# The end of the hybrid layer: gate projection in its own group, norm factor in the last scan step, three more attention units in written order

## The chip, the cores and the metric

One core of a Trainium2 chip runs the whole program. The metric is the device time of one execution in microseconds (us); several executions are given by their median. The engines are named as the profile names them: PE (TensorE, matmuls), DVE (VectorE), ACT (ScalarE), POOL (GpSimd) and SP (SyncE, which issues most DMAs).

## What is computed

Two layers act on 512 latent tokens and 256 context tokens of width 1024. The first layer (hybrid) has two branches that share one input and one output projection: a bidirectional state-space scan of 16 heads in 4 groups, and a 2-D neighbourhood attention of 8 heads, which the kernel takes in 4 pairs. The second layer is a differential attention. Each layer ends in a gated MLP. The change is in the hybrid layer alone:

```python
def hybrid_mixer(ux, uc, w_in, ..., w_out, with_ctx):
    z_x, xbc_x, dt_x, q_x, k_x, v_x = parts(ux @ w_in)
    z_c, xbc_c, dt_c, q_c, k_c, v_c = parts(uc @ w_in)
    y_x, y_c = ssd_branch(...)
    a_x = neighbourhood_attention(q_x, k_x, v_x, k_c, v_c, rpb)
    ox = concatenate([y_x, a_x]) @ w_out

def gate_norm(y, z):                       # end of ssd_branch
    y = y.reshape(b, n, SSD_INNER) * silu(z)
    return rms_norm(y, norm_w)             # y * rsqrt(mean(y*y) + eps) * norm_w
```

The scan works in 6 chunks of 128 tokens (4 latent, 2 context). A chunk's output is a decay-weighted product inside the chunk plus what the states before it bring in from either direction.

## The kernel before

Weights are fp32. `wchunk` (line 156) loads a piece, ACT writes its high part and DVE (or POOL) its low part, and every dense product is three matmuls: high by high, high by the input's low part, low by high. On PE these show as px and pc (128x512 latent and 128x256 context columns, `ct_x`, `ct_c`, line 328), pz (the gate, `tc_mm`, line 344) and po (the output projection).

The hybrid layer is written as four rounds, one for a group g of four scan heads. In a round `run` takes the generators of `gens` in turn, one step each: `ssd_group(g)`, the scan, and from round 1 on `na_pair(g - 1)`, an attention pair of six units of 128 queries. After every second turn it takes one step of the filler, the dense work of later groups: `dense_ssd(g + 1)`, `x_rows(g + 1)`, `dense_na(g)` and `dense_z(g + 1)`, in this order. In round 3 the filler is `dense_na(3)` and `early()`, which loads the finished scan output (yr), transposes it (ytp), splits it in high and low parts (act tiles) and starts the output projection. The writing order gives each instruction a priority; a scheduler then orders each engine's queue by it, so that filler stands where the scan and the attention wait. What the filler of round 3 issues has its priority lowered by 4000.

One step of the scan (lines 673 to 712) reads a tile E of decays that POOL has loaded (`load_E`: a DMA, line 649, and two selects, lines 650 and 652), takes eight exponentials on ACT (line 681), eight products with dt on DVE (684, 685) and a product with the chunk's C B matrix (688, called M below), and then the four matmuls of line 706, which are called the chunk's products below. E, the scan's states, the inputs of the layer (`u`, 12 tiles) and the act tiles (12) share one pool, `blk`, of 18 buffers; so three are left for E in a round, and act tiles can be had only as E tiles and `u` come free. Line 711 squares and sums the gated output into ssq.

An attention unit (`na_unit`) makes scores on PE, adds the bias and takes the maximum on DVE, the exponential on ACT, the reciprocal and the scaling on DVE, the transposes on PE (line 108, S<-P), their copies on ACT or DVE (Pt, line 788) and the product with V on PE. Units 0 to 3 are latent, 4 and 5 context.

After the four rounds the norm factor rr is made (lines 949 to 952: a sum and a scale on DVE, a square root on ACT, a reciprocal and a scale on DVE). Then pair 3 runs with PE's order written out by hand (`pe.chain = True`): its q and k are split (`split_qk`, lines 746 to 752, to which five tiles of one buffer each belong) and V is transposed, and then each unit's three stages alternate with one `piece()`, that is one step of `rest()`: a group of 18 po matmuls and its evacuation by DVE and POOL.

Of the kernel before, what the change touches and what calls it, by code (L numbers as in the profile page):

```python
# [10 lines left out]
F32 = mybir.dt.float32  # L11
# [3 lines left out]
OP = mybir.AluOpType  # L15
# [59 lines left out]
def emit(tc, T):  # L75
# [546 lines left out]
    def ssd_group(g, BC, xs):  # L622
        Bc, Cc = BC
        hs = slice(4 * g, 4 * g + 4)
        Bt = sp.tile([128, 6, 128], F32, name="Bt", bufs=1)
        for c0, cn in ((0, 4), (4, 2)):
            p = pss.tile([128, 4, 128], F32, name="btp", tag="ax")
            for c in range(cn):
                nc.tensor.transpose(p[:, c], Bc[:, 128 * (c0 + c):128 * (c0 + c) + 128], ident)
            nc.scalar.copy(Bt[:, c0:c0 + cn], p[:, 0:cn])  # L630
        yield
        PVb = [blk.tile([128, 2, 2, 4, 64], F32, name="PV", tag="b") for _ in range(3)]
        PV = [PVb[k // 2][:, k % 2] for k in range(5)]
        wsg = wst.rearrange("p c (d h) -> p c d h", d=2)
        sdg = sd.rearrange("p c (d h) -> p c d h", d=2)
        b4 = [128, 2, 4, 64]

        def scaled(c, w, name, eng):
            xd = sp.tile([128, 2, 4, 64], F32, name=name, tag="f2", bufs=4)
            eng.tensor_tensor(xd, xs[c].rearrange("p (h q) -> p h q", q=64).unsqueeze(1).to_broadcast(b4),  # L640
                              w[:, c, :, hs].unsqueeze(3).to_broadcast(b4), op=OP.mult)
            return xd

        Es = {}

        def load_E(c):
            E = blk.tile([128, 2, 4, 128], F32, name="E", tag="b")
            base = scr[g, c].rearrange("d h l -> (d h l)")
            nc.gpsimd.dma_start(E.rearrange("p d h l -> p (d h l)"), base.unsqueeze(0).to_broadcast([128, 1024]))
            nc.gpsimd.affine_select(out=E[:, 0], in_=E[:, 0], pattern=[[0, 4], [1, 128]], compare_op=OP.is_ge,  # L650
                                    fill=NEG, base=0, channel_multiplier=-1)
            nc.gpsimd.affine_select(out=E[:, 1], in_=E[:, 1], pattern=[[0, 4], [-1, 128]], compare_op=OP.is_ge,
                                    fill=NEG, base=0, channel_multiplier=1)
            Es[c] = E

        for c in FO[:E_AHEAD[g]]:
            load_E(c)

        xw = {}
        for k in range(5):  # L660
            for c in (FO[k], BO[k]):
                if c not in xw:
                    xw[c] = scaled(c, wsg, "xw", nc.gpsimd)
            p = pss.tile([128, 2, 256], F32, name="Sps", tag="ax")
            nc.tensor.matmul(p[:, 0], Bt[:, FO[k]], xw[FO[k]][:, 0].rearrange("p h q -> p (h q)"), start=True, stop=True)
            nc.tensor.matmul(p[:, 1], Bt[:, BO[k]], xw[BO[k]][:, 1].rearrange("p h q -> p (h q)"), start=True, stop=True)
            pv = PV[k].rearrange("p d h q -> p d (h q)")
            if k == 0:
                nc.scalar.copy(pv, p)
            else:  # L670
                nc.gpsimd.tensor_tensor(PV[k], PV[k - 1], cdk[:, k, :, hs].unsqueeze(3).to_broadcast(b4), op=OP.mult)
                nc.vector.tensor_tensor(pv, pv, p, op=OP.add)
            yield
        for c in (4, 5, 0, 1, 2, 3):
            if c not in Es:
                load_E(c)
            E = Es.pop(c)
            for d in range(2):
                for h in range(4):
                    i = 16 * d + 4 * g + h  # L680
                    nc.scalar.activation(E[:, d, h], E[:, d, h], AF.Exp, bias=acs[:, c, i:i + 1])
            M = E[:, 0]
            for h in range(4):
                nc.vector.tensor_scalar(E[:, 1, h], E[:, 1, h], dt[:, c, 16 + 4 * g + h:17 + 4 * g + h], None, op0=OP.mult)
                nc.vector.scalar_tensor_tensor(M[:, h], M[:, h], dt[:, c, 4 * g + h:4 * g + h + 1], E[:, 1, h], op0=OP.mult, op1=OP.add)
            gp = pss.tile([128, 512], F32, name="gp", tag="ax")
            nc.tensor.matmul(gp[:, 0:128], Bc[:, 128 * c:128 * c + 128], Cc[:, 128 * c:128 * c + 128], start=True, stop=True)
            nc.vector.tensor_tensor(M, M, gp[:, 0:128].unsqueeze(1).to_broadcast([128, 4, 128]), op=OP.mult)
            kf, kb = FO.index(c), BO.index(c)
            op_ = pss.tile([128, 2, 256], F32, name="op", tag="ax")  # L690
            t1 = sp.tile([128, 2, 4, 64], F32, name="t1", tag="f2", bufs=4)
            ds_ = [d for d, k in ((0, kf), (1, kb)) if k > 0]
            for d in ds_:
                k = (kf, kb)[d]
                nc.tensor.matmul(op_[:, d], Cc[:, 128 * c:128 * c + 128], PV[k - 1][:, d].rearrange("p h q -> p (h q)"), start=True, stop=True)
            d0, d1 = ds_[0], ds_[-1] + 1
            nc.vector.tensor_tensor(t1[:, d0:d1], op_[:, d0:d1].rearrange("p d (h q) -> p d h q", q=64),
                                    sdg[:, c, d0:d1, hs].unsqueeze(3).to_broadcast([128, d1 - d0, 4, 64]), op=OP.mult)
            xD = sp.tile([128, 4, 64], F32, name="xD", tag="xD", bufs=2)
            nc.gpsimd.tensor_tensor(xD, xs[c].rearrange("p (h q) -> p h q", q=64),  # L700
                                    dsum[:, hs].unsqueeze(2).to_broadcast([128, 4, 64]), op=OP.mult)
            for d in ds_:
                nc.gpsimd.tensor_tensor(xD, xD, t1[:, d], op=OP.add)
            dg = gp[:, 128:384].rearrange("p (h q) -> p h q", q=64)
            for h in range(4):
                nc.tensor.matmul(dg[:, h], M[:, h], xs[c][:, 64 * h:64 * h + 64], start=True, stop=True)
            nc.vector.tensor_tensor(xD, xD, dg, op=OP.add)
            yf = xD.rearrange("p h q -> p (h q)")
            nc.vector.tensor_tensor(yf, yf, zs.pop((g, c)), op=OP.mult)
            nc.gpsimd.dma_start(scrY[c, :, 256 * g:256 * g + 256], yf)  # L710
            nc.scalar.activation(t1[:, 0].rearrange("p h q -> p (h q)"), yf, AF.Square, accum_out=ssq[:, c, g:g + 1])
            yield


# [45 lines left out]
    def na_unit(Q, Kh, Kl, V, qo, k0, chunks, bias, out, pool, tp_, nb, split=False):  # L760
# [55 lines left out]
                pe.matmul(av[hp], V[0:m, c, hp], Ss[e][1][0:m, i], start=(i == 0), stop=(i == len(chunks) - 1))  # L816
        out(av)

    def na_values(v):
        V = np_.tile([128, 7, 128], F32, name="V")  # L820
        for grp in ((1, 2, 3, 5), (6, 0, 4)):
# [22 lines left out]
            return na_unit(*QK, V, 128 * k, k0, chunks + (5, 6), bt, lambda av: na_out(p, 128 * k, av), pool, tp_, nb, split)  # L844
        return na_unit(*QK, V, 128 * k, None, (5, 6), None, lambda av: na_out(p, 128 * k, av), pool, tp_, nb, split)

    def na_pair(p, q, k, v, pools, nb=2):
        QK = split_qk(q, k)
        V = na_values(v)
        yield  # L850
        for u_ in range(6):
            bt = na_bias(p, u_, np_, nb) if u_ < 4 else None
            for _ in na_one(p, u_, QK, V, bt, pools[u_ % 4 % len(pools)], np_, nb):
                pass
            yield
# [19 lines left out]
    PNA = (pna, "na")  # L875
    dense, densen, rows, zs = {}, {}, {}, {}
    bg[:] = [(0, w, h) for w in (2, 4, 3) for h in range(2)]
    for _ in chain(dense_ssd(0), dense_z(0), x_rows(0)):
        pass
    acts, atts, Yt, pend = {}, {}, {}, []  # L880

# [48 lines left out]
    for g in range(4):  # L930
# [1 line left out]
            pmm.seq = MM  # L932
        gens = [ssd_group(g, *rows[g])]
        if g > 0:
            gens.append(na_pair(g - 1, *densen[g - 1], [(nring, None) if g == 3 else PNA]))
        fl = []
        if g < 3:
            fl += [dense_ssd(g + 1), x_rows(g + 1)]
        fl.append(dense_na(g))
        if g < 3:  # L940
            fl.append(dense_z(g + 1))
        if g == 3:
            fl.append(early())
        run(gens, chain(*fl), 4000 if g == 3 else 0)
# [1 line left out]
    pmm.seq = MM + [(pm3, "mm")]  # L946
    while bg:
        fill()
    ssr = sp.tile([128, 6], F32, name="ssr")
    nc.vector.tensor_reduce(ssr, ssq, axis=AX, op=OP.add)  # L950
    nc.vector.tensor_scalar(ssr, ssr, 1.0 / D, RMS_EPS, op0=OP.mult, op1=OP.add)
    nc.vector.tensor_scalar(rr, rsqrt_(ssr, sp), 1.0 / ALPHA, None, op0=OP.mult)
    s1.close()
    s4 = ExitStack()
    op4 = s4.enter_context(tc.tile_pool(name="op4", bufs=1))
# [67 lines left out]
    def piece():  # L1023
        pr = tc.cur_priority
        tc.cur_priority = pr + 4000
        next(rs_, None)
        tc.cur_priority = pr

    bts = [na_bias(3, b, np2, 4) for b in range(2)]
    QK3 = split_qk(*N[:2])  # L1030
    V3 = na_values(N[2])
    for tt in range(6):
        load_res(tt)
    evac_y()
    pe.chain = True
    prev = None
    for k in range(6):
        if 0 < k < 3:
            bts.append(na_bias(3, k + 1, np2, 4))
        un = na_one(3, k, QK3, V3, bts[k] if k < 4 else None, (PNA, (pss, "ax"))[k % 2], np2, 4, True)  # L1040
        next(un)
        if prev is not None:
            next(prev)
        piece()
        if prev is not None:
            next(prev, None)
        prev = un
# [518 lines left out]
```

## Time and profile before

| | |
|---|---|
| median of 3 runs | 2026.2 us (2025.8 to 2028.28) |
| the profiled execution's own time | 2025.07 us |
| its span | 2023.3 us |
| PE busy | 1920.8 us (95%) |
| DVE, ACT, POOL busy | 1352.1, 920.5, 769.6 us |
| chain that ended last | PE 72%, DVE 12%, DMA, POOL and ACT 4% each |

PE is busy nearly everywhere, so time can be won only where it is idle or runs at a low granted clock. The page's 40 slices show such places at the start, at some 490 to 560 us (the end of the hybrid layer) and at 700 to 760 us (the start of the first MLP). A view of the windows gives these stretches one by one.

### The profile page before, as it was taken

How to read it: one execution, taken by the hardware profiler on the slowest of the kernel's cores; microseconds unless marked ns; L12 is line 12 of the kernel's file. 1: busy time of each engine (PE TensorE's matmuls, PEld its weight loads, DVE VectorE, ACT ScalarE, POOL GpSimd, SP SyncE). 2: the span in 40 equal slices, each digit the busy share in tenths (PEclk: the TensorE clock that was granted, in tenths of full speed). 3: DMA queues.
4: the chain of work that ended last, by engine and by line, in shares of the span. 5: the costliest groups of instructions: out<-in, count | busy, mean ns of one | idle time of the engine just before them, and what ended most of it. 6: DMA issues, size and time to landing. Idle time of an engine off the chain costs nothing.

```text
span 2023.3 us, 31146 instructions
## 1 busy us (share of the span) xinstructions
PE 1920.8 (95%) x11928; PEld 1645.3 (81%) x11928; DVE 1352.1 (67%) x2172; ACT 920.5 (45%) x1799; POOL 769.6 (38%) x658
## 2 busy tenths in 40 slices
PE   7998999998699889999999999899999899999997
PEld 5887889887477788878888888899998788888886
DVE  3757565765556887887676667566665876655566
ACT  3545466585442732323222234656665644333332
POOL 2135224336315675444444408431115264222133
PEclk9999999999699989999999999999999999999999
DMA  9335342233422243433343342222122223323321
GB/s 314 113 114 170 110 129 76 96 117 117 155 68 88 87 135 100 130 116 115 105 144 106 104 135 86 92 73 85 55 66 68 89 64 126 104 84 104 103 96 62
DMA packets 109445, 217.59 MB, mean 108 GB/s; under 512 B 27112, under 2 KB 45904, under 8 KB 109296
## 3 DMA queue, kind: packets, MB, share of 16 engines
q1 hardware_dynamic: 95168, 187.87, 28.9%
q0 software_dynamic: 6016, 20.03, 2.8%
q10 hardware_dynamic: 8112, 7.71, 1.3%
q8 instruction: 94, 1.54, 0.3%
q14 instruction: 55, 0.45, 0.1%
HBM read 202.81 MB, written 8.55 MB: 104 GB/s over the span
## 4 chain that ended last, share of the span: by engine, by line
PE 72%; DVE 12%; DMA 4%; POOL 4%; ACT 4%; issue 3%; ACTq 0%; SPq 0%; DVEq 0%; POOLq 0%
PE fpx L328 20%; PE pdn L1122 11%; PE px L328 7%; PE fpc L328 5%; PE S L108 3%; PE po L108 3%; PE pc L328 3%; PE pz L344 3%; DVE acc L223 2%; PE pv L344 2%; DMA araw<-in_ada_w 2%; POOL y L409 2%; PE dSp L1329 2%; PE po L1005 2%; PE pk L328 2%
## 5 line engine op out<-in xcount | busy, mean ns | idle before, releaser
L172 ACT ACTIVATE whi<-raw 128x1024 fp32r<-128x1024 f32 (+1 forms) x203 | 213.4, 1056 | 443.5 <-PE fpc L328 167.2
L173 DVE TENSOR_TENSOR wlo<-raw,whi 128x1024 fp32r<-128x1024 f32 (+1 forms) x190 | 251.8, 1330 | 157.4 <-ACT whi L172 144.6
L352 POOL TENSOR_TENSOR y<-y,ev 128x512 f32<-128x512 f32 x144 | 212.5, 1495 | 185.1 <-DVE ev L350 175.2
L1122 PE MATMUL pdn<-whi,fact 128*128 128x512 f32 x880 | 273.1, 392 | 2.1 <-DVE ev L350 1.8
L328 PE MATMUL fpx<-ux,whi 128*128 128x512 f32 (+1 forms) x832 | 232.3, 363 | 8.2 <-DVE cv L1081 7.6
L328 PE MATMUL fpx<-u,whi 128*128 128x512 f32 (+1 forms) x832 | 226.5, 358 | 2.4 <-DVE cv L1081 1.5
L1122 PEld LDWEIGHTS pdn<-whi,fact 128*128 128x128 f32 x880 | 162.4, 188 | 37.2 <-DVE ev L350 2.9
L328 PEld LDWEIGHTS fpx<-ux,whi 128*128 128x128 f32 x832 | 150.3, 194 | 31.1 <-ACT whi L172 8.0
L1122 PE MATMUL pdn<-wlo,fact 128*128 128x512 f32 x440 | 170.8, 390 | 0.7 <-DVE wlo L173 0.7
L328 PEld LDWEIGHTS fpx<-u,whi 128*128 128x128 f32 x832 | 149.2, 191 | 25.1 <-ACT cv L1077 1.6
L328 PE MATMUL fpx<-ux,wlo 128*128 128x512 f32 (+1 forms) x416 | 151.1, 364 | 8.5 <-POOL wlo L173 6.6
L223 DVE SCALAR_TENSOR_TENSOR acc<-araw,condp,acc 128x512 f32<-128x512 f32 x140 | 137.4, 1002 | 24.4 <-DMA araw<-in_ada_w 24.0
L1106 POOL TENSOR_TENSOR fact<-cv,fact 128x768 fp32r<-128x768 f32 (+1 forms) x44 | 70.6, 1605 | 217.5 <-ACT fact L1105 217.5
L328 PE MATMUL fpx<-u,wlo 128*128 128x512 f32 (+1 forms) x416 | 148.8, 358 | 1.1 <-DVE wlo L173 1.1
L328 PE MATMUL px<-ux,whi 128*128 128x512 f32 x448 | 148.5, 405 | 0.0
L171 POOL TENSOR_TENSOR raw<-raw,G 128x1024 f32<-128x1024 f32 x30 | 74.4, 2482 | 193.0 <-DMA raw<-in_w_down 113.0
L1081 DVE SCALAR_TENSOR_TENSOR cv<-fpx,fcw,cv 128x511 f32<-128x511 f32 x176 | 130.3, 744 | 20.8 <-ACT cv L1077 19.6
L328 PE MATMUL fpc<-uc,whi 128*128 128x256 f32 x704 | 130.2, 283 | 0.0
L328 PEld LDWEIGHTS fpc<-uc,whi 128*128 128x128 f32 x704 | 112.6, 191 | 4.2 <-issue 0.6
L409 POOL TENSOR_TENSOR y<-y,gb 128x256 f32<-128x256 f32 x112 | 98.9, 918 | 35.2 <-PE lntp L388 28.7
L1077 ACT ACTIVATE cv<-fpx,fcw 128x512 f32<-128x512 f32 x88 | 67.8, 771 | 80.7 <-PE fpx L328 76.5
L350 DVE SCALAR_TENSOR_TENSOR ev<-pdn,G 128x512 f32<-128x512 f32 x120 | 81.3, 683 | 32.0 <-POOL y L352 18.9
(335 smaller groups left out, 4628.0 us busy)
## 6 DMA issues: line engine op xcount, KB each, us to landing
araw<-in_ada_w SPq DMA_DIRECT2D x96, 512.0 KB
raw<-in_w_up SPq DMA_DIRECT2D x88, 512.0 KB
raw<-in_w_down SPq DMA_DIRECT2D x44, 512.0 KB
E<-scr POOLq DMA_DIRECT2D x24, 512.0 KB, 5.4
raw<-in_w_dqk SPq DMA_DIRECT2D x16, 512.0 KB
raw<-in_w_qkv SPq DMA_DIRECT2D x12, 512.0 KB
raw<-in_w_out SPq DMA_DIRECT2D x12, 512.0 KB
raw<-in_w_bc SPq DMA_DIRECT2D x8, 512.0 KB
```

What stands on the lines that cost most here:

```text
L108: i = f(*a, **k)
L171: nc.gpsimd.tensor_tensor(raw, raw, gate, op=OP.mult)
L172: nc.scalar.activation(hi[:, :n], raw[:, :n], AF.Copy)
L173: i = (eng or nc.vector).tensor_tensor(lo[:, :n], raw[:, :n], hi[:, :n].bitcast(F32), op=OP.subtract)
L223: nc.vector.scalar_tensor_tensor(acc[:, s], raw[:, i], cs, acc[:, s], op0=OP.mult, op1=OP.add)
L328: nc.tensor.matmul(ps, w[wi][:, kc], rhs(kc, ui), start=(i == 0), stop=(i == n - 1))
L344: nc.tensor.matmul(ps, u_dst(u, kc, ui, tt), w(kc, wi), start=(i == 0), stop=(i == n - 1))
L350: nc.vector.scalar_tensor_tensor(t, ps, r, Gh, op0=OP.mult, op1=OP.mult)
L352: eng.tensor_tensor(yh, yh, t, op=OP.add)
L409: i = nc.gpsimd.tensor_tensor(y[:, c:c + 256], y[:, c:c + 256], t[:, c:c + 256], op=op)
L1081: nc.vector.scalar_tensor_tensor(dst[:, lo:hi_], src[:, lo + d:hi_ + d], f[:, tap:tap + 1], dst[:, lo:hi_], op0=OP.mult, op1=OP.add)
L1122: nc.tensor.matmul(ps, acts[2 * gs[0] + kt][:, ui, 128 * tt:128 * tt + 128], ws[kt][wi][:, 0, o:o + 512], start=(m == 0), stop=(m == 3 * n ...
```

## The change

Four edits, all in the hybrid layer.

- The gate's projection of a group, `dense_z(g)`, is the first filler of round g instead of the last filler of round g - 1. The sequence of the filler is the same; what moves is where the rounds' scans and attention pairs begin against it. In round 3 this leaves `dense_z(3)`, `dense_na(3)` and `early()`.
- The norm factor is written inside the last step of the last scan instead of behind the rounds.
- Pair 2 runs only its units 0 to 2 in round 3 (`n=3`); units 3 to 5 run behind the rounds in the order written out by hand, ahead of pair 3, each with the stages split and a `piece()` between them.
- The split of pair 3's q and k and the transposes of its V come between the two pairs, with a `piece()` on either side, instead of ahead of all.

```diff
--- before.py
+++ after.py
@@ -709,6 +709,11 @@
             nc.vector.tensor_tensor(yf, yf, zs.pop((g, c)), op=OP.mult)
             nc.gpsimd.dma_start(scrY[c, :, 256 * g:256 * g + 256], yf)
             nc.scalar.activation(t1[:, 0].rearrange("p h q -> p (h q)"), yf, AF.Square, accum_out=ssq[:, c, g:g + 1])
+            if g == 3 and c == 3:
+                ssr = sp.tile([128, 6], F32, name="ssr")
+                nc.vector.tensor_reduce(ssr, ssq, axis=AX, op=OP.add)
+                nc.vector.tensor_scalar(ssr, ssr, 1.0 / D, RMS_EPS, op0=OP.mult, op1=OP.add)
+                nc.vector.tensor_scalar(rr, rsqrt_(ssr, sp), 1.0 / ALPHA, None, op0=OP.mult)
             yield
 
 
@@ -816,6 +821,8 @@
                 pe.matmul(av[hp], V[0:m, c, hp], Ss[e][1][0:m, i], start=(i == 0), stop=(i == len(chunks) - 1))
         out(av)
 
+    held = {}
+
     def na_values(v):
         V = np_.tile([128, 7, 128], F32, name="V")
         for grp in ((1, 2, 3, 5), (6, 0, 4)):
@@ -844,11 +851,12 @@
             return na_unit(*QK, V, 128 * k, k0, chunks + (5, 6), bt, lambda av: na_out(p, 128 * k, av), pool, tp_, nb, split)
         return na_unit(*QK, V, 128 * k, None, (5, 6), None, lambda av: na_out(p, 128 * k, av), pool, tp_, nb, split)
 
-    def na_pair(p, q, k, v, pools, nb=2):
+    def na_pair(p, q, k, v, pools, nb=2, n=6):
         QK = split_qk(q, k)
         V = na_values(v)
+        held[p] = QK, V
         yield
-        for u_ in range(6):
+        for u_ in range(n):
             bt = na_bias(p, u_, np_, nb) if u_ < 4 else None
             for _ in na_one(p, u_, QK, V, bt, pools[u_ % 4 % len(pools)], np_, nb):
                 pass
@@ -875,7 +883,7 @@
     PNA = (pna, "na")
     dense, densen, rows, zs = {}, {}, {}, {}
     bg[:] = [(0, w, h) for w in (2, 4, 3) for h in range(2)]
-    for _ in chain(dense_ssd(0), dense_z(0), x_rows(0)):
+    for _ in chain(dense_ssd(0), x_rows(0)):
         pass
     acts, atts, Yt, pend = {}, {}, {}, []
 
@@ -932,13 +940,11 @@
             pmm.seq = MM
         gens = [ssd_group(g, *rows[g])]
         if g > 0:
-            gens.append(na_pair(g - 1, *densen[g - 1], [(nring, None) if g == 3 else PNA]))
-        fl = []
+            gens.append(na_pair(g - 1, *densen[g - 1], [(nring, None) if g == 3 else PNA], n=3 if g == 3 else 6))
+        fl = [dense_z(g)]
         if g < 3:
             fl += [dense_ssd(g + 1), x_rows(g + 1)]
         fl.append(dense_na(g))
-        if g < 3:
-            fl.append(dense_z(g + 1))
         if g == 3:
             fl.append(early())
         run(gens, chain(*fl), 4000 if g == 3 else 0)
@@ -946,10 +952,6 @@
     pmm.seq = MM + [(pm3, "mm")]
     while bg:
         fill()
-    ssr = sp.tile([128, 6], F32, name="ssr")
-    nc.vector.tensor_reduce(ssr, ssq, axis=AX, op=OP.add)
-    nc.vector.tensor_scalar(ssr, ssr, 1.0 / D, RMS_EPS, op0=OP.mult, op1=OP.add)
-    nc.vector.tensor_scalar(rr, rsqrt_(ssr, sp), 1.0 / ALPHA, None, op0=OP.mult)
     s1.close()
     s4 = ExitStack()
     op4 = s4.enter_context(tc.tile_pool(name="op4", bufs=1))
@@ -1026,22 +1028,33 @@
         next(rs_, None)
         tc.cur_priority = pr
 
+    two = (PNA, (pss, "ax"))
+    bt2 = na_bias(2, 3, np_, 2)
+    late = [lambda k=k: na_one(2, k, *held[2], bt2 if k == 3 else None, two[k % 2], np_, 2, True) for k in (3, 4, 5)]
     bts = [na_bias(3, b, np2, 4) for b in range(2)]
-    QK3 = split_qk(*N[:2])
-    V3 = na_values(N[2])
     for tt in range(6):
         load_res(tt)
     evac_y()
     pe.chain = True
     prev = None
-    for k in range(6):
+    for n_, make in enumerate(late + list(range(6))):
+        if n_ == 3:
+            next(prev)
+            piece()
+            next(prev, None)
+            prev = None
+            QK3 = split_qk(*N[:2])
+            V3 = na_values(N[2])
+            piece()
+        k = n_ - 3
         if 0 < k < 3:
             bts.append(na_bias(3, k + 1, np2, 4))
-        un = na_one(3, k, QK3, V3, bts[k] if k < 4 else None, (PNA, (pss, "ax"))[k % 2], np2, 4, True)
+        un = make() if n_ < 3 else na_one(3, k, QK3, V3, bts[k] if k < 4 else None, two[k % 2], np2, 4, True)
         next(un)
         if prev is not None:
             next(prev)
-        piece()
+        if n_:
+            piece()
         if prev is not None:
             next(prev, None)
         prev = un
```

How instructions move. In the rows below S is the attention's scores tile, written by the score matmuls (from nKh, nKl and nQ, whose numbers tell the pairs apart), by the transposes (from P) and by the product with V (from Pt); gp of line 706 is the chunk's product; xtp, btp and vtp are transposes of the scan's x and B and of V.

First place: PE in round 0, around the products of the scan. Before, the first chunk's products and those behind it stood apart by dense work:

```order
L615 MATMUL xtp<-c_consts,xt 128x128 x2
L706 MATMUL gp<-xs,E 128x64 x4
L328 MATMUL pc<-uc,whi 128x256 x2
L328 MATMUL pc<-uc,wlo 128x256
L328 MATMUL pc<-uc,whi 128x256 x2
L328 MATMUL pc<-uc,wlo 128x256
L328 MATMUL pc<-uc,whi 128x256 x2
L328 MATMUL pc<-uc,wlo 128x256
```

and now the last chunks of the same scan:

```order
L328 MATMUL px<-ux,whi 128x512 x2
L328 MATMUL px<-ux,wlo 128x512 x2
L695 MATMUL op<-PV,xc 128x256 x2
L687 MATMUL gp<-xc 128x128
L695 MATMUL op<-PV,xc 128x256 x2
L706 MATMUL gp<-xs,E 128x64 x8
L687 MATMUL gp<-xc 128x128
L695 MATMUL op<-PV,xc 128x256 x2
L706 MATMUL gp<-xs,E 128x64 x4
L629 MATMUL btp<-c_consts,xc 128x128 x6
L328 MATMUL px<-ux,whi 128x512 x2
```

Between a round's first and last product there were 48 px, 72 pc and 37 pz in round 0, and now there are 25 px; the six chunks stand in three rows (x12 for three chunks, further up; x8 for two, x4 for one).

Second place: PE in round 3, the middle of the last scan. Before:

```order
L108 MATMUL ytp<-c_consts,yr 128x128 x4
L108 MATMUL S<-nKh_4854,nQ_4857 128x512
L687 MATMUL gp<-xc 128x128
L695 MATMUL op<-PV,xc 128x256 x2
L108 MATMUL ytp<-c_consts,yr 128x128 x6
L687 MATMUL gp<-xc 128x128
L695 MATMUL op<-PV,xc 128x256 x2
L108 MATMUL ytp<-c_consts,yr 128x128 x2
L706 MATMUL gp<-xs,E 128x64 x8
L108 MATMUL S<-c_consts,P 128x128 x4
L687 MATMUL gp<-xc 128x128
L108 MATMUL S<-c_consts,P 128x128 x4
```

and now:

```order
L328 MATMUL px<-ux,whi 128x512
L108 MATMUL S<-Pt,V 64x128 x7
L706 MATMUL gp<-xs,E 128x64 x4
L687 MATMUL gp<-xc 128x128
L695 MATMUL op<-PV,xc 128x256 x2
L328 MATMUL px<-ux,whi 128x512
L328 MATMUL px<-ux,wlo 128x512
L328 MATMUL px<-ux,whi 128x512 x2
L328 MATMUL px<-ux,wlo 128x512
L328 MATMUL pc<-uc,whi 128x256 x2
L328 MATMUL pc<-uc,wlo 128x256
```

Before, the dense work of round 3 had ended (4 pc are left behind the first product), and the scan was mixed with the transposes ytp; now 31 px and 46 pc stand between its first and last product, and ytp begins behind them. Between the first state product (Sps) and the last product of this scan there were 24 px and 35 pc, and there are 53 px and 70 pc.

Third place: PE behind the last scan, units 4 and 5 of pair 2. Before, they followed each other and pair 3's first unit with no dense work between:

```order
L108 MATMUL S<-c_consts,P 128x128 x4
L108 MATMUL S<-Pt,V 64x128 x4
L108 MATMUL vtp<-c_consts,v 128x128 x4
L108 MATMUL S<-nKh_4855,nQ_4858 128x256
L108 MATMUL S<-nKl,nQ_4857 128x256
L108 MATMUL S<-nKl,nQ_4858 128x256
L108 MATMUL S<-c_consts,P 128x128 x4
L108 MATMUL S<-Pt,V 64x128 x4
L108 MATMUL vtp<-c_consts,v 128x128
L108 MATMUL vtp<-c_consts,v 64x128 x2
L108 MATMUL S<-nKh_5831,nQ_5834 128x512
L108 MATMUL S<-nKh_5832,nQ_5835 128x512
```

and now (the row that follows is the first of 54 po):

```order
L108 MATMUL S<-Pt,V 64x128 x8
L108 MATMUL S<-nKh_4689,nQ_4692 128x256
L108 MATMUL S<-nKh_4690,nQ_4693 128x256
L108 MATMUL S<-nKl,nQ_4692 128x256
L108 MATMUL S<-nKl,nQ_4693 128x256
L108 MATMUL S<-c_consts,P 128x128 x4
L108 MATMUL ytp<-c_consts,yr 128x128 x12
L108 MATMUL po<-whi,act_5535 128x512
```

Behind these come 54 po, unit 4's product with V, unit 5's transposes, 18 po, unit 5's product, V's transposes, 18 po, and pair 3's first scores. One group of 18 po stands ahead of the rows shown. On ACT, at the same place, the act tiles (from ytp) stood between the last scan's exponentials and squares:

```order
L681 ACTIVATE E<-E,acs 128x128 x4
L893 CAST act_5697<-ytp 128x512
L711 ACTIVATE t_5469,ssq<-xD 128x256
L681 ACTIVATE E<-E,acs 128x128 x4
L895 COPY yr<-ytp 128x512
L893 CAST act_5697<-ytp 128x256
L834 DMA scrA<-att 128x128
L895 COPY yr<-ytp 128x256
```

and now most of them stand behind these, between the attention's copies and the split of pair 3:

```order
L901 CAST act_5589<-ytp 128x512
L903 COPY yr<-ytp 128x512
L901 CAST act_5589<-ytp 128x256
L903 COPY yr<-ytp 128x256
L840 COPY att<-S 128x128
L753 CAST nKh_5915<-k 64x768
L753 CAST nKh_5916<-k 64x768
L841 DMA scrA<-att 128x128
L754 CAST nQ_5918<-q 64x768
L805 ACTIVATE P,nm<-S,nm 128x256
L754 CAST nQ_5919<-q 64x768
L756 CAST nKh_5915<-nKh_5915 64x768
L805 ACTIVATE P,nm<-S,nm 128x256
L901 CAST act_5607<-ytp 128x512
```

In ACT's queue from the copies of unit 2's transposes to the last act tile there are now five and a half of the six token tiles' casts and copies, units 3 to 5, the square root with a table load on either side, and the split of pair 3.

## Rows read from the trace of the kernel before

**Rows 1.** Windows: length; busy us of PE, PEld, DVE, ACT, POOL; granted clock, DMA, GB/s.
```profile
100.00:200.00 100.00, 92.69 (x704) 79.82 (x702) 65.33 (x125) 53.51 (x116) 47.70 (x59) 0.98 0.45 144
200.00:433.00 233.00, 231.99 (x1622) 200.41 (x1623) 148.87 (x330) 144.36 (x325) 78.49 (x103) 1.00 0.35 110
...
461.60:482.00 20.40, 20.40 (x125) 17.06 (x124) 10.46 (x21) 10.06 (x28) 12.83 (x16) 1.00 0.25 91
482.00:516.50 34.50, 25.03 (x133) 19.67 (x132) 28.71 (x66) 22.66 (x68) 23.80 (x30) 0.78 0.38 130
516.50:565.40 48.90, 34.75 (x150) 23.92 (x149) 23.26 (x49) 22.21 (x60) 12.56 (x11) 0.66 0.49 161
```

**Rows 2.** PE's waits from 461 to 566: who for whom, total, times, longest.
```profile
PE S L108 <- DVE P L802: 11.7, 3, 9.3
```

**Rows 3.** PE's timeline, 540 to 560: start, us, operation, idle before and its releaser.
```profile
553.91 1.08 PE L108 MATMUL S<-c_consts,P 128*128 128x128 f32 x4 [9.29 <-DVE P L802]
```

**Rows 4.** DVE's timeline at the same place.
```profile
545.00 2.10 DVE L291 TENSOR_TENSOR G<-G,grow 128x512 f32<-128x512 f32 x1
...
549.34 3.84 DVE L750 TENSOR_TENSOR nQ<-q,nQ 64x768 fp32r<-64x768 f32 x2
```

**Rows 5.** The chain that ended last, 440 to 570: start, us, what.
```profile
442.91 5.01 PE px L328 x22
...
449.05 2.02 PE pc L328 x17
...
560.12 5.71 PE po L108 x18
```

**Rows 6.** DVE's timeline: M of the first and last chunk, in rounds 0 and 3.
```profile
144.71 0.68 DVE L688 TENSOR_TENSOR E<-E,gp 128x512 f32<-128x512 f32 x1
...
194.41 0.68 DVE L688 TENSOR_TENSOR E<-E,gp 128x512 f32<-128x512 f32 x1
...
474.90 0.69 DVE L688 TENSOR_TENSOR E<-E,gp 128x512 f32<-128x512 f32 x1
...
513.61 0.67 DVE L688 TENSOR_TENSOR E<-E,gp 128x512 f32<-128x512 f32 x1
```

**Rows 7.** The tile E: durations in ns (min/median/max), and its loads from issue to landing.
```profile
L684 DVE TENSOR_SCALAR E<-E,dt x96: 271/280/1844, 141.7 to 510.2; 128x128 f32<-128x128 f32 x96
...
L652 POOL TENSOR_SCALAR_AFFINE_SELECT E<-E x24: 624/629/1670, 136.4 to 498.3; 128x512 f32<-128x512 f32 x24
...
DMA to landing us min/median/max: 3.6/5.4/8.2
```

**Rows 8.** ACT's timeline: the eight exponentials of a chunk in round 0.
```profile
139.53 2.45 ACT L681 ACTIVATE E<-E,acs 128x128 f32<-128x128 f32 x8
```

**Rows 9.** ACT's groups by form, 482 to 566: count, busy us, mean ns, idle before.
```profile
L800 ACT ACTIVATION_READ_ACCUMULATOR P<-S,nm 128x1 f32 x12 | 2.4, 196 | 0.0
L895 ACT COPY yr<-ytp 128x512 f32<-128x512 f32 x6 | 3.5, 590 | 0.0
L893 ACT CAST act<-ytp 128x512 fp32r<-128x512 f32 x6 | 3.5, 584 | 1.8 <-PE ytp L108 1.8
...
L895 ACT COPY yr<-ytp 128x256 f32<-128x256 f32 x6 | 2.3, 391 | 0.0
...
L893 ACT CAST act<-ytp 128x256 fp32r<-128x256 f32 x6 | 2.3, 376 | 0.0
...
L800 ACT ACTIVATE P<-S,nm 128x256 f32<-128x256 f32 x4 | 1.9, 468 | 1.2 <-DVE nm L799 1.2
...
L749 ACT CAST nQ<-q 64x768 fp32r<-64x768 f32 x2 | 1.7, 830 | 0.0
...
L298 ACT ACT_TABLE_LOAD x1 | 1.3, 1283 | 0.0
...
L800 ACT ACTIVATE P<-S,nm 128x448 f32<-128x448 f32 x2 | 1.3, 634 | 3.8 <-DVE ssr L951 3.8
```

**Rows 10.** POOL's and PE's timeline at the start of the first MLP.
```profile
679.67 24.63 POOL L409 TENSOR_TENSOR y<-y,gb 128x256 f32<-128x256 f32 x28 [4.56 <-ACT ux L401]
...
707.10 0.58 PE L328 MATMUL fpx<-ux,wlo 128*128 128x256 f32 x1 [6.58 <-POOL wlo L173]
```

## The prediction

> **What bounds it now.** I read the windows first [rows 1]: for each stretch its length, PE's busy time and the granted clock, that is the share of TensorE's full level (2.4 GHz; the low one is 1.2). Length less busy time times clock is what a stretch loses. From 200 to 433 us it loses 1.0 and from 461.6 to 482 nothing: there PE is the bound, and no engine beside it is worth anything. The end of the hybrid layer loses 34.5 - 25.03 x 0.78 = 15.0 from 482 to 516.5, and 48.9 - 34.75 x 0.66 = 26.0 from 516.5 to 565.4: **41 us** together. From 100 to 200, mostly round 0's scan, it loses 100 - 92.69 x 0.98 = 9.2. These places are what the change touches.
>
> Next the waits at the end. The largest is PE's for the softmax tile P, 11.7 us in three, one of 9.3 [rows 2]; PE's timeline shows it at 553.9, before unit 5's transposes [rows 3]. DVE's timeline says why: ahead of that P in DVE's queue stand sums for the gates (2.10) and the split of pair 3's q (3.84) [rows 4]. That split can't run early, since its tiles have one buffer each and unit 5's scores still read pair 2's. The matmuls that come after, the first po, took 5.71 us for 18 [rows 5]; at the rate of the px ahead of them, 5.01/22 = 0.228 us each, it would be 4.1. So the idle time costs another 1.6 in clock.
>
> The scan is slow without cover: from its first to its last M it took 38.7 us in round 3, where almost no dense work was left, and 49.7 in round 0, where 48 px, 72 pc and 37 pz stood in it [rows 6].
>
> **The change by parts.**
>
> *The gate's projection moved.* No instruction is added; against the same row of dense work the rounds start earlier. The last scan gains cover: between its first state product and its last product 53 px + 70 pc in place of 24 + 35, at 0.228 and 0.119 us (2.02/17) [rows 5] 20.4 us for 9.7. Rounds 1 and 2 keep 48 px, 65 pc, 8 pz and 61 px, 48 pc, 16 pz between first and last product: 19.6 and 21.5 (a pz taken like a pc). Round 0 keeps only 25 px: 5.7 for 23.9 (48 x 0.228 + 109 x 0.119). Adding PE's own scan and attention work, by my estimate about 10 to 13 us (under half of the 25.03 that PE was busy at the last scan [rows 1], which had more attention and ytp), the cover from first to last product is about 15, 33, 36 and 26 us in rounds 0 to 3.
>
> What must be covered? One chunk's way through its tile E is a load (5.4), two selects (0.63 each) and eight products with dt (8 x 0.28) [rows 7], eight exponentials (2.45) [rows 8] and M (0.68) [rows 6]: 12.0 with nothing in the way. Three buffers serve six chunks, so two waves, of which the first load comes early: I take **25 us** from first to last. The bounds: 5/3 of 12.0, that is 20, and the 38.7 measured. By 25, round 0 loses 25 - 15 = 10 inside the scan and, I estimate, half of today's 9.2 around it, so 15 for 9.2: **+6**. Bounds: -9 if nothing is lost, +15 if it needs 38.7. Rounds 1 and 2: **+2** for disorder (0 to 9). Round 3 keeps 3, counted below.
>
> *The norm factor.* The same five instructions and two table loads of 1.283 [rows 9] stay on ACT around one square root; they move past a few instructions. The reload stands in front of unit 3's exponential, whose row today names the norm's ssr as what it waited for (3.8) [rows 9]. I count nothing by itself; the two loads are in ACT's sum below.
>
> *Pair 2's last units, and the act tiles.* What goes is the wait at 553.9: the split of pair 3 now stands behind unit 5, and po stands between the units. What is late next is ACT. In its queue from the copies of unit 2's transposes to the last act tile stand [rows 9]:
> - act tiles, 5.4 token tiles x (0.590 + 0.584 + 0.391 + 0.376): 10.5
> - pair 3's split, 6 x 0.83: 5.0
> - two table loads and the root: 2.8
> - exponentials with their readout, 2 x (0.634 + 0.196) + 4 x (0.468 + 0.196): 4.3
> - copies of transposes, attention outputs and a square, about 11 at some 0.4 (estimate, as the copy of 128 x 256): 4.5
>
> Sum 27.1. The 54 po stand in PE's queue behind all ytp, so behind this. PE has beside it one group of po (4.1) and the units' and ytp matmuls, about 10 (estimate: a sixth of the 59.8 it was busy in these two windows, the rest stands elsewhere now). So 13 idle, 1.6 at low clock on restart as above, 3 for the end of scan 3, 2 for going back and forth between units: the new loss is about **20** where 41 stood. Bounds: 10, if half of ACT's 27 runs early, under the scan, whose window left ACT 34.5 - 22.66 = 11.8 us idle [rows 1]; 33, if it all comes late and pair 3's preparation, now in the middle, waits as well.
>
> *Queues.* The act tiles need buffers that E and `u` free, and yr comes through two buffers, so SP's loads for a token tile wait for POOL's low part two tiles before. The order is kept, all of it is later, and the 20 holds it. At the first MLP POOL has 30 instead of 28 row operations ahead of its first low part, 24.63/28 = 0.88 each, and PE waits there for it, 6.58 today [rows 10]: **+1.5** (0 to 2).
>
> **Sum:** -41 + 20 + 6 + 2 + 1.5 = -11.5. The profiled execution took 2025.07 (span 2023.3), 1.1 below the median of 2026.2; 2025.1 - 11.5 = 2013.6, so **2014 us**.
>
> **Rivals.** What a measurement of this kernel can tell from no change is about 0.2%, 4 us.
>
> *A, the end is nearly all covered.* ACT's act tiles run in its idle time under the last scan, the end loses 10, round 0 nothing more than now: -41 + 10 + 1.5 = -29.5, some 1996. For it: those 11.8 us. Against: act tiles need buffers from E, so they come behind the scan.
>
> *B, it nets out.* The end is a chain through ACT, DVE and PE in which each unit's step waits behind tiles or the split, and it loses 30 and not 20: -1.5, some 2024. For it: ACT's queue puts the split's casts between unit 5's exponentials and act tiles; the place of the wait changes from DVE to ACT and its size little.
>
> *C, slower: the scan's own pace.* If a scan needs 38.7 us whatever stands beside it, the rounds lose 24, 6, 3 and 13 (46) for the 15 that I took (10, 2, 0, 3): +31, some 2045. At 36 it is 21, 3, 0, 10: +19, 2033. It comes out slower than now from a pace of some 33 to 34 on. For it: 38.7 is what was measured with PE idle. Against: that scan shared ACT and DVE with three attention units and act tiles, and DVE was busy 28.71 of 34.5 us [rows 1]; round 0's has none of these. The row shows DVE at 28.71 and POOL at 23.80 in 34.5 us, so they worked side by side for at least 18.0; yet single selects and products with dt took 1.67 and 1.84 where 0.63 and 0.28 are usual [rows 7].
>
> The Trainium skill's page "SBUF — State Buffer", section "Who interferes with whom", says that VectorE and GpSimd share one pair of ports as an exclusive lock, and the loser stands still for the whole instruction. Were that so for every pair of theirs, the two could not pack 28.71 + 23.80 = 52.5 us into less, and C would be near certain; the trace disagrees for most pairs (18.0 us side by side) and agrees for the few long ones. (The page restricts the lock to some VectorE instructions; which of these they are no row says.)
>
> *D, the moves don't do what they say.* The orders of the engines show the dense work and units moved as described; only the norm factor does nothing by itself. I give this no chance of its own.
>
> **How the numbers follow.** The forecast (2005 to 2022) 0.48, A 0.12, B 0.20, C 0.20. Faster by over 0.2% is the forecast and A, 0.60; within 0.2% is B, 0.20; slower is C, 0.20. The forecast's own bounds are those of its terms; to leave out no more than 2 in 10, the range takes in B and the near parts of A and C: 1998 to 2035.
>
> **What would show it.** Right: a window from the last scan to pair 3's first scores that loses some 20; no wait for P of several us there; ACT back to back ahead of the long run of po; a PE idle of some 10 us before products of round 0's scan; E's pace there near 25 from first to last M; POOL's low part at the first MLP awaited 1.5 longer. Wrong: a scan that takes over 33 us with PE idle in it (C), PE's waits at the end on ACT of 25 us or more (B), or a full clock there (A).

## The result, and the profile after

The changed kernel took 2038.7 us (median of 5 runs, 2034.9 to 2041.2), the kernel before 2028.3 beside it: a ratio of 1.0054, interval 1.0039 to 1.0069. It is **slower by half a per cent**, above the range of 1998 to 2035, and on the other side of zero than forecast. The profiled execution took 2041.2 (span 2039.4), so it shows 16.1 us more than the one of before, where the medians differ by 10.4.

The windows of the changed kernel, columns as in [rows 1]:

```profile
100.00:200.00 100.00, 86.51 (x545) 73.45 (x543) 57.11 (x125) 45.24 (x106) 43.65 (x60) 0.86 0.38 120
200.00:300.00 100.00, 94.81 (x702) 80.49 (x701) 64.18 (x139) 60.63 (x133) 38.67 (x46) 0.95 0.43 138
300.00:400.00 100.00, 98.18 (x680) 83.58 (x679) 62.86 (x138) 62.78 (x141) 38.87 (x48) 1.00 0.30 97
480.00:520.00 40.00, 38.14 (x245) 31.94 (x245) 35.56 (x69) 21.54 (x68) 21.35 (x32) 0.98 0.34 108
520.00:560.00 40.00, 29.18 (x162) 22.00 (x162) 27.07 (x55) 27.23 (x66) 19.39 (x20) 0.89 0.56 185
560.00:600.00 40.00, 36.85 (x183) 28.16 (x182) 21.97 (x40) 13.55 (x38) 11.75 (x10) 0.91 0.39 129
```

By length less busy time times clock, the last three lose 2.6, 14.0 and 6.5: the end improved about as forecast. The first two lose 25.6 and 9.9, where [rows 1] gives 9.2 and, for 200 to 433, 1.0: the early rounds got slower.

PE's waits at the end, where [rows 2] had 11.7 us for the tile P:

```profile
PE ytp L108 <- ACT yr L903: 3.7, 1, 3.7
...
PE po L108 <- ACT yr L903: 1.9, 1, 1.9
PE ytp L108 <- DMA yr<-scrY: 1.7, 1, 1.7
PE S L108 <- DVE P L807: 1.6, 1, 1.6
```

P is down to 1.6, and what is late now is ACT's copies of the act tiles (line 903). The chain of waits (start, us, what) has the 54 po in one piece behind them, at 0.26 us each:

```profile
552.66 14.17 PE po L108 x54
```

Round 0 is where the time went. DVE's timeline, M of the first and third, then of the fourth and sixth chunk (before: [rows 6]):

```profile
130.26 0.68 DVE L688 TENSOR_TENSOR E<-E,gp 128x512 f32<-128x512 f32 x1
...
134.52 0.69 DVE L688 TENSOR_TENSOR E<-E,gp 128x512 f32<-128x512 f32 x1
...
155.91 0.68 DVE L688 TENSOR_TENSOR E<-E,gp 128x512 f32<-128x512 f32 x1
...
163.20 0.67 DVE L688 TENSOR_TENSOR E<-E,gp 128x512 f32<-128x512 f32 x1
```

Two waves are to be seen: three chunks within 4.3 us, a gap of 21.4, three more within 7.3. From first to last it is 32.9. The chain of waits tells what fills the gap:

```profile
129.54 7.02 PE px L328 x23
136.56 0.85 PE gp L706 x8
137.43 0.43 DVE xD L707
137.93 6.42 DMA E<-scr
144.43 1.28 ACT L681
```

The first three M were there by 135.2, the first by 130.9; but their products stood in PE's queue behind 23 px and ran at 136.56, together. So all three buffers came free one right behind the other, and POOL, which issues the loads, had stood still 11.26 us for the first (the view names xD, DVE's sum behind the first product); the three loads went out within 2 us:

```profile
137.93 0.58 POOL L649 DMA_DIRECT2D E<-scr  x1 [11.26 <-DVE xD L707]
...
144.41 0.63 POOL L650 TENSOR_SCALAR_AFFINE_SELECT E<-E 128x512 f32<-128x512 f32 x1 [3.46 <-DMA E<-scr]
```

ACT then took the exponentials of three chunks in one row, after a table load, and DVE their products with dt behind them:

```profile
145.73 7.12 ACT L681 ACTIVATE E<-E,acs 128x128 f32<-128x128 f32 x24
```

```profile
149.07 1.63 DVE L173 TENSOR_TENSOR wlo<-raw,whi 128x1024 fp32r<-128x1024 f32 x1
150.62 0.74 DVE L684 TENSOR_SCALAR E<-E,dt 128x128 f32<-128x128 f32 x1
...
152.21 0.68 DVE L697 TENSOR_TENSOR t<-op,sd 128x512 f32<-128x512 f32 x1
```

PE meanwhile stood at the next chunk, and what it did from 150 to 170 us ran at the low level of its clock. DVE, third of the busy columns, worked without a gap there:

```profile
152.95 0.80 PE L687 MATMUL gp<-xc 128*128 128x128 f32 x2 [5.98 <-DVE t L697]
```

```profile
150.00:160.00 10.00, 5.01 (x18) 4.36 (x18) 10.00 (x27) 4.95 (x15) 4.28 (x5) 0.50 0.20 66
160.00:170.00 10.00, 8.40 (x29) 6.64 (x29) 10.00 (x21) 4.53 (x16) 7.13 (x11) 0.50 0.17 66
```

### The profile page after: what moved, and what is told of

The parts are those of the page before. It is cut to its first block, busy times and chain, and to the rows that moved or that the text cites. A ratio compares the mean times of both kernels' runs of the same rounds, so it can differ in the third digit from the quotient of the medians.

```text
span 2039.4 us, 31146 instructions
## 1 busy us (share of the span) xinstructions
PE 1928.7 (95%) x11928; PEld 1649.6 (81%) x11928; DVE 1355.3 (66%) x2175; ACT 918.2 (45%) x1796; POOL 775.0 (38%) x658
## 4 chain that ended last, share of the span: by engine, by line
PE 69%; DVE 13%; DMA 5%; POOL 5%; issue 4%; ACT 4%; SPq 0%; ACTq 0%; DVEq 0%; POOLq 0%
PE fpx L328 20%; PE pdn L1135 11%; PE px L328 6%; PE fpc L328 5%; PE pc L328 3%; PE po L108 3%; PE pv L344 2%; PE pz L344 2%; DVE acc L223 2%; DMA araw<-in_ada_w 2%; POOL y L409 2%; PE S L108 2%; PE pk L328 2%; PE avp L1363 2%; PE dSp L1342 2%
## 5 line engine op out<-in xcount | busy, mean ns | idle before, releaser
L328 PEld LDWEIGHTS fpx<-u,whi 128*128 128x128 f32 x832 | 148.0, 189 | 26.1 <-ACT cv L1090 2.3
L328 PE MATMUL fpx<-ux,wlo 128*128 128x512 f32 (+1 forms) x416 | 150.8, 363 | 11.4 <-POOL wlo L173 6.5
L328 PE MATMUL px<-ux,whi 128*128 128x512 f32 x448 | 153.1, 417 | 1.7 <-ACT whi L172 1.0
L1094 DVE SCALAR_TENSOR_TENSOR cv<-fpx,fcw,cv 128x511 f32<-128x511 f32 x176 | 130.4, 744 | 22.0 <-ACT cv L1090 20.8
```

What stands on the lines that cost most here:

```text
L328: nc.tensor.matmul(ps, w[wi][:, kc], rhs(kc, ui), start=(i == 0), stop=(i == n - 1))
L1094: nc.vector.scalar_tensor_tensor(dst[:, lo:hi_], src[:, lo + d:hi_ + d], f[:, tap:tap + 1], dst[:, lo:hi_], op0=OP.mult, op1=OP.add)
```

## The experiments

Two theories to begin with. T: the gate's projection took cover from the early scans, which lose their own pace less the cover. R1: the moved units and queues are the loss. The table sums each kernel's losses by stage, each window's length less busy time times clock (windows of 100 us, but one of 80 from 400 to 480 and three of 40 from 480 to 600). The losses are of one profiled execution each, which lies up to 5.8 us from its kernel's median (g2), and in a slower kernel the later stages stand later in the windows:

| kernel | median us | 100-200 | 200-400 | 400-480 | 480-600 | 600-800 | 800-1400 |
|---|---|---|---|---|---|---|---|
| before | 2028.3 | 9.2 | 1.0 | 1.7 | 40.9 | 24.6 | 14.2 |
| changed | 2038.7 | 25.6 | 11.7 | 0.0 | 23.1 | 24.7 | 21.3 |
| e1, gate as before | 2019.9 | 9.5 | 1.0 | 1.3 | 29.5 | 28.3 | 13.7 |
| e2, gate moved alone | 2041.9 | 24.9 | 11.8 | 0.0 | 30.7 | 23.6 | 21.6 |
| e3, gate of group 3 moved | 2025.1 | 10.6 | 1.0 | 5.6 | 24.0 | 26.8 | 16.7 |
| e4, norm factor back | 2037.8 | 25.1 | 9.3 | 0.0 | 23.0 | 24.1 | 20.1 |
| g1, gate of group 0 back | 2023.3 | 9.3 | 8.0 | 0.0 | 21.4 | 27.2 | 18.2 |
| g2, gate of group 0 moved | 2033.3 | 26.0 | 1.2 | 1.7 | 35.9 | 24.9 | 13.8 |
| f1, step's order | 2039.4 | 25.4 | 10.1 | 0.8 | 20.8 | 25.1 | 22.8 |
| f2, six E | 2040.6 | 15.5 | 7.2 | 7.3 | 30.2 | 24.6 | 20.6 |
| f4, e1 and step's order | 2017.6 | 8.9 | 1.4 | 0.0 | 27.5 | 26.1 | 17.9 |
| f3, no products with dt in round 0 | 2034.5 | 4.9 | 12.7 | 4.0 | 31.9 | 26.5 | 20.7 |
| g3, f4 and six E | 2007.2 | 7.8 | 1.8 | 0.0 | 18.1 | 24.7 | 14.0 |
| h1, before with f1's order and six E | 2019.3 | 7.9 | 1.6 | 0.0 | 28.3 | 25.5 | 17.7 |

The kernel before ran beside each set, with medians of 2026.9 to 2029.1; ratios below are to these runs.

**The parts of the change.** e1 puts the gate's projection back, in the changed kernel:

```diff
-    for _ in chain(dense_ssd(0), x_rows(0)):
+    for _ in chain(dense_ssd(0), dense_z(0), x_rows(0)):
...
-        fl = [dense_z(g)]
+        fl = []
...
         fl.append(dense_na(g))
+        if g < 3:
+            fl.append(dense_z(g + 1))
```

> The change with the gate's projection put back to the end of the round before, all else kept. Theory T (the early scans lost their cover: rounds 0 to 2 lose 37 us in the changed kernel's profile, 10 before): those 27 us come back, the last scan gets its old cover and loses some 10 more than in the changed kernel: about 2022 us, faster than the change by 15 or more, and the stretch from 100 to 200 us loses 9 to 10. Rival R1 (the loss comes from the moved units and queues, and the gate's projection matters little): within 5 us of the changed kernel's 2039.

2019.9 us, ratio to before 0.9956 (0.9942 to 0.9971). R1 falls: without the gate's move the change is faster than before. e2 is the kernel before with the opposite edit alone:

> The kernel before with the gate's projection moved, nothing else. T: rounds 0 to 2 lose 25 to 27 us more, the last scan gains some 12, the wait for the tile P at the end stays: 2038 to 2045 us, slower than before by 0.6% or more. R1: within 5 us of before, or faster by the last scan's 12.

2041.9, ratio 1.0070 (1.0052 to 1.0088). So the two edits stand with opposite signs: the moved units (with the norm factor) bring 8.5, the moved gate costs 13.6, and both together cost 10.4, some 5 more than the sum.

> The change with only the last group's gate projection in its own round; groups 0 to 2 as before. T: rounds 0 and 1 as before, round 2 loses up to 5 us, the end keeps the changed kernel's gain of 18: 2008 to 2014 us, faster than both. Rival R2 (round 2's scan pays for it as round 0's did): 2020 to 2026.

The edit moves `dense_z(3)` alone into round 3 (`fl = [dense_z(3)] if g == 3 else []`, the others as in e1). 2025.1, ratio 0.9987 (0.9975 to 0.9999): T's number missed, 5 worse than e1. But R2's reason is not shown either: round 2's end, 400 to 480, loses 4.3 more than in e1, and the last scan has hardly more cover (12.3 lost from 480 to 520, 16.1 in e1). In PE's order the scheduler drew 63 pz of the group into round 2 all the same, since filler stands wherever a scan waits; so the run hardly prices the move of group 3's gate.

> The change with the norm factor behind the rounds again. T: within 4 us of the changed kernel (2035 to 2043), since the same five instructions move past a few others. Rival R3 (the square root's two table loads and the new wait on ACT in the last step hold up the end): faster than the change by 5 or more.

2037.8, ratio 1.0051 (1.0032 to 1.0070): the norm factor's place makes no difference that can be told, and R3 falls.

**Which round pays.** g1 keeps the gate of group 0 ahead of round 0 in the changed kernel (`fl = [dense_z(g)] if g > 0 else []`); g2 moves that of group 0 alone in e1.

> The change with group 0's gate projection alone put back ahead of round 0; groups 1 to 3 in their own rounds. Theory T (each scan loses about its own 33 us less its cover, each round for itself): 100 to 200 us loses 9 to 10 as before, round 1 some 10 to 15 as its cover is about that of the change, the end stays at the change's 23: 2021 to 2028. Rival G (what round 0 gives back is lost again in later rounds, as with six buffers): within 4 us of the change's 2039.

> The version with the gate's projection as before and the attention units moved (2020 us), with group 0's gate projection alone moved into round 0. T: 100 to 200 us loses 24 to 26, round 1 about 1, the last scan its 16 as before: 2033 to 2040. G: within 4 us of 2020, or beyond 2045.

2023.3 (0.9968, 0.9950 to 0.9985) and 2033.3 (1.0021, 1.0004 to 1.0039), both within T, at g2's lower edge. Group 0's move costs 15.4 where the other groups' moves are made too (2038.7 - 2023.3), 13.4 where they are not (2033.3 - 2019.9), and 100 to 200 us shows it: 9.3 and 9.5 against 25.6 and 26.0. The other three groups' moves cost 3.4 to 5.4 together. (g2's last scan stands some 22 us later than e1's, so their columns from 400 to 800 don't compare one by one.) g1's round 1 lost less than T gave (8.0 for 10 to 15).

**What sets a scan's pace.** f1 writes the state products and their scaling ahead of the exponentials, in the changed kernel:

```diff
-            for d in range(2):
-                for h in range(4):
-                    i = 16 * d + 4 * g + h
-                    nc.scalar.activation(E[:, d, h], E[:, d, h], AF.Exp, bias=acs[:, c, i:i + 1])
...
             for d in ds_:
                 nc.gpsimd.tensor_tensor(xD, xD, t1[:, d], op=OP.add)
+            for d in range(2):
+                for h in range(4):
+                    i = 16 * d + 4 * g + h
+                    nc.scalar.activation(E[:, d, h], E[:, d, h], AF.Exp, bias=acs[:, c, i:i + 1])
...
```

> The change with the scan's step written in another order: the state products and their scaling (op, t, xD) ahead of the exponentials and the products with dt, so that on DVE the scaling t no longer stands behind the next tiles' products. Theory Q (round 0's loss of 25.6 us comes largely from DVE's order, since PE waited 6.0 us for t): round 0 loses 17 to 20, total 2031 to 2034. Theory W (a scan's six chunks go in two waves of three buffers, and the second wave is late whatever DVE's order): round 0 loses 23 or more, total within 4 us of 2039.

2039.4, ratio 1.0068 (1.0043 to 1.0094), and round 0 loses 25.4: DVE's order is not the cause, though PE's longest wait names it. Q falls. f2 gives E six buffers in round 0:

```diff
+            if g == 0 and c in (1, 2, 3):
+                tags = (("nKh0", "nKh1"), ("nKl", "nQ0"), ("nQ1", "V"))[c - 1]
+                E = [np_.tile([128, 4, 128], F32, name="E2", tag=t) for t in tags]
...
```

> The change with six buffers for the tile E in round 0 instead of three (the last three chunks take memory of attention tiles that are not in use yet; their loads are two halves each). W: the second wave starts with the first, the last M comes 8 to 15 us earlier, 100 to 200 us loses 10 to 17 where it was 25.6, total 2024 to 2031. Rival P (six chunks in series on ACT, 6 x 2.45, and on DVE, 6 x 3.6, set the pace): 100 to 200 us still loses 21 or more, total within 4 us of 2039.

Half of W: the first and last M are 27.9 us apart and no longer come in two clusters,

```profile
137.96 0.69 DVE L696 TENSOR_TENSOR E<-E,gp 128x512 f32<-128x512 f32 x1
143.31 0.69 DVE L696 TENSOR_TENSOR E<-E,gp 128x512 f32<-128x512 f32 x1
...
165.90 0.68 DVE L696 TENSOR_TENSOR E<-E,gp 128x512 f32<-128x512 f32 x1
```

and 100 to 200 us loses 15.5 for 25.6, where P asked for 21 or more. But the first M is 7.7 later and the last 2.7 later, not earlier as W has it, and the total did not move (2040.6, ratio 1.0074, 1.0051 to 1.0097). The gain is lost again at 400 to 480 (7.3) and 480 to 600 (7.1 more); there PE's largest wait is a load of the scan's output:

```profile
PE ytp L108 <- DMA yr<-scrY: 8.6, 1, 8.6
```

f3 leaves out the products with dt in round 0 (`for h in range(4 if g else 0)`).

> The change with the eight products with dt left out in round 0 (some 2.5 us of DVE a chunk; that part of the computation is not done). P: DVE's 15 us less shorten round 0 by 8 or more: 100 to 200 us loses under 18. W: by 2 to 6, as only one chunk's products lie in each wave's own chain: it loses 19 to 24.

One execution, 2034.5: 100 to 200 us loses 4.9, as P would have it. How much of the scan's pace is DVE's own work stays open all the same: P is not told from W here, since the scheduler put other work between: 64 px and 23 pc stand between first and last product now, where there were 25 px, and the M are still 30.3 apart (32.9). The gain went again: 31.9 lost from 480 to 600.

**Towards a better version.** f4 is e1 with f1's order, g3 that with f2's six buffers.

> The version with the gate's projection as before and the attention units moved, with the scan's step in the other order too. Q: the last scan, which lost 16 us from 480 to 520, loses 8 to 12, total 2010 to 2016, the fastest so far. W: within 4 us of 2020.

2017.6, ratio 0.9953 (0.9935 to 0.9971), beside e1's 0.9956: the order alone is worth nothing that can be told, and Q is wrong here too.

> The version with the gate's projection as before, the attention units moved and the scan's step in the other order (2017.6 us), with six buffers for E in round 0. T: round 0 loses 9 there, of which some 3 wait for DMA; it gains up to 6: 2011 to 2016, the fastest. G: the gain is lost again later: within 4 us of 2018.

**2007.2, ratio 0.9878 (0.9857 to 0.9899)**, the fastest of all. M in round 0, first and last:

```profile
148.51 0.67 DVE L711 TENSOR_TENSOR E<-E,gp 128x512 f32<-128x512 f32 x1
...
173.36 0.68 DVE L711 TENSOR_TENSOR E<-E,gp 128x512 f32<-128x512 f32 x1
```

24.9 us apart for f4's 49.1. The total bears T's expectation out and more, but not its place: 100 to 200 us gained only 1.1; the end gained 9.4 and 800 to 1400 us 3.9. Why these did is open. Round 0 itself splits in two. By narrower windows, from 140 to 200 us, where its M lie, f4 loses 7.2 and g3 nothing, so the scan is fully covered; but from 100 to 140 g3 loses 8.1 (f4: 1.5), since PE waits there 4.4 us for the scan's states. First f4, then g3 twice:

```profile
140.00:200.00 60.00, 54.40 (x440) 47.18 (x439) 45.13 (x95) 39.62 (x94) 29.03 (x38) 0.97 0.49 160
...
100.00:140.00 40.00, 35.01 (x233) 28.93 (x232) 23.59 (x51) 20.78 (x43) 20.25 (x27) 0.91 0.48 143
140.00:200.00 60.00, 60.00 (x492) 53.45 (x491) 40.51 (x77) 36.21 (x80) 30.08 (x38) 1.00 0.46 147
```

A last run puts the same two edits on the kernel before:

> The kernel before with six buffers for E in round 0 and the scan's step in the other order, the attention units and the gate's projection as before. If these two bring what they brought beside the moved units (2019.9 to 2007.2, some 12.7), it takes 2013 to 2018, and the moved units are worth 6 to 11 in the best version. If the 12.7 hung on the moved units, within 4 us of before (2022 to 2031).

2019.3, ratio 0.9953 (0.9938 to 0.9968), a little above the first case: order and buffers bring 9.6 there, and the moved units 12.1 beside them (2019.3 - 2007.2).

## Why the prediction was wrong

**The step that failed** is the sentence "I take 25 us from first to last" for a scan's pace, the larger of the terms behind the +6 and +2. I had put one chunk's way through E (12.0) for a wave. Measured is 32.9 in round 0 and 37.6, 41.0 and 33.5 in rounds 1 to 3 (first to last M). A wave is a chunk's way plus two more chunks in series: exponentials 7.12 for three in place of 2.45, a table load of 1.28 ahead, products with dt of three on DVE. DVE had no idle time in the second wave, and its queue held other work between them: a weight's low part (1.63) and some 2.6 us of the next group's x (line 566) before the last M. And I gave no time to the products' place in PE's in-order queue, which held the first wave's buffers till 137.4 and later, though the first M was done at 130.9. With six buffers round 0's scan takes 24.9 (g3) and 27.9 (f2): the 25 was the pace of a scan that has no second wave. The 12.0 itself read all eight products with dt at 0.28; the four of line 685 take 0.34 in the kernel before. That adds 0.25 and is not what failed:

```profile
L685 DVE SCALAR_TENSOR_TENSOR E<-E,dt x96: 327/343/1444, 142.1 to 511.6; 128x128 f32<-128x128 f32 x96
```

By terms:

- *Round 0*, forecast +6 with bounds of -9 and +15: measured +16.4 (9.2 to 25.6), over the upper bound. That bound leaves out the 4.6 around the scan which the +6 holds; with it, 38.7 gives +19. e2, g1 and g2 show that group 0's gate alone does it. PE's idle time from 100 to 200 grew by 6.2 only (7.3 to 13.5); the other 9 to 10, by the width of the windows, are busy time at the low level of the clock. The forecast has a term for that at the end (1.6) and none in round 0. Whether the low level also made the scan longer, or ran in time that PE would have waited, no run here separates.
- *Rounds 1 and 2*, forecast +2 (0 to 9): +10.7 (1.0 to 11.7). The cover was as I had it; the pace was not.
- *The end*, forecast 41 to 20 and with it -21: -17.8 from 480 to 600 and -1.7 from 400 to 480, so -19.5. Right in size and in its reason: the wait for P went, ACT's copies are what is late, and the po ran in one piece behind them. There is luck in the size: of the 13 us idle behind ACT, PE's waits on ACT show 7.6 (3.7 and 1.9 above, three more of 2.0 together), and 6.0 of the 23.1 lie behind pair 3's first scores (577.6 on), where nothing was forecast. Each part does about half by itself: the moved units 11.4 without the gate (e1, 40.9 to 29.5), the gate 10.2 without them (e2, 40.9 to 30.7).
- *Norm factor*, nothing: right (e4).
- *First MLP*, forecast +1.5: wrong by a little. POOL has its 30 row operations there and PE waits 6.50 us, as before with 6.58 [rows 10]; 600 to 800 lost 24.7 for 24.6.

```profile
718.97 0.58 PE L328 MATMUL fpx<-ux,wlo 128*128 128x256 f32 x1 [6.50 <-POOL wlo L173]
```

- *Not foreseen*: 800 to 1400 us loses 7.1 more. The six kernels with all four gates moved show 20.1 to 22.8 there, the others 13.7 to 18.2, g2 with group 0's alone among them (13.8). What passes it on I can't say.

These sum to +14.8 of the 16.1 that the profiled executions differ by. Windows of 10 us over the whole span keep idle time and low clock better apart; by them the changed kernel loses 12.0 more (131.5 to 143.5), and less, not more, behind 1400 us. The other 4.1 is PE's busy time times clock, and where it comes from is open.

**Rival C** was the true case, with its condition named (a pace from 33 to 34 on) and a chance of 0.20. Its price fits: by the covers of the forecast the measured spans leave 18, 5, 5 and 7, some 20 more than I took, which gives 2034; the 7.1 behind 800 us are in no rival. I gave the 38.7 too little weight, because that scan ran beside attention and act tiles; round 0 has none of these, and took 32.9 all the same.

The rule of the Trainium skill on the shared ports ("SBUF — State Buffer", "Who interferes with whom") I had weighed lightly by the 18.0 us side by side. In the second wave single products with dt took 0.74 where 0.28 is usual [rows 7], while POOL's sums ran long too, two in 2.63, where one by itself takes 0.72 to 0.74 elsewhere in that scan:

```profile
149.58 2.63 POOL L703 TENSOR_TENSOR xD<-xD,t 128x256 f32<-128x256 f32 x2
```

These rows agree with the rule. What the scan would take without it no run here tries.

## What to carry to other kernels

A chain that runs in waves through few buffers is costed by the wave: the latency of one member, plus the others in series on the slowest engine, plus the time that the releasing instruction stands in its in-order queue. Work that covers such a chain has a price at the place that it leaves, and this is greatest where nothing else runs beside the chain, as in the first round. And where a scheduler orders the queues, a gain in one stage counts only when the whole program is timed: here the same six buffers brought 10 us in round 0 and nothing in total, or 10 in total and 1 from 100 to 200 us.

## What was not expected of the hardware

From 150 to 170 us the granted clock was 0.50, the low level, while PE was busy 5.01 and 8.40 us of 10. So of the 25.6 lost from 100 to 200, 6.7 are busy time at the low level in this stretch and not idle time. PE had been busy 6.97 us of the ten before, at 1.00.
